# Projecting the S5 input blocks in pairs, and zeroing the far probabilities' tiles on VectorE

## The chip, the cores and the metric

One core of one Trainium2 chip runs the kernel. The metric is the time of one execution on the device in microseconds (us), as the median of several runs. The engines are named as in the profile: PE is TensorE's matmuls and PEld its weight loads, DVE is VectorE, ACT is ScalarE, POOL is GpSimd, SP is the engine that issues most of the loads. "PEq", "SPq" and so on are the sequencers of these engines.

## What is computed

A decoder trunk of two layers over 1024 positions of width 1024, in fp32. Layer 0 projects its normed input once and feeds 16 heads of dilated attention and a multi-scale pooling; layer 1 feeds a chunked spatial gating unit and an S5 state-space layer. After each mixer comes a cross-attention into 256 memory tokens. Cut to what the change touches:

```python
# layer 0: attention, a mixture of three (window, dilation) patterns
A_PATTERNS = ((128, 1), (512, 4), (2048, 16))
a_out = dilated_attention(q, k, v) * silu(g_a)
# layer 1
hn = rms_norm(x, norm_cd)
u_c, v_c, g_c, x_d, g_d = split(hn @ w_in_cd)          # x_d: 512 channels
c_out = spatial_gating(u_c, v_c, ...) * silu(g_c)
d_out = s5_ssm(x_d, ...) * silu(g_d)                    # per group of 16 channels a complex state of 64
y = concatenate([c_out, d_out]) @ w_out_cd
```

## The kernel before

Activations lie with channels on the partitions and 1024 positions on the free axis, in two halves of 512. Every fp32 operand of a large product is split into a rounded part and a rest (`hilo`, and `split` for weights), and each product is three matmuls (`mm3`, L206 to L208). A projection (`proj`) of one block of 128 output channels over one half is 8 x 3 matmuls of 128x512 into one PSUM tile; the PSUM tags have two buffers each ("mm", "s", "o", "t"). An RMS norm is not applied to the input of a projection: the gain is, and the scale 1/rms of each half, `R[0]` and `R[1]`, is multiplied in when the projection is evicted. The sum for the scale is formed by two matmuls with ones (`norm_sum_pe`, L310 and L311), and VectorE then computes the scale by three Newton steps (`norm_sum_end`, `rsqrt`, L289 to L293).

Weights are loaded by SP in the order of a plan (`plan`), split by ACT and DVE some places ahead (`pump`, counted from the oldest weight in use), and freed after their second half (`proj` with h = 1). SBUF tiles come from rings that are shared by many names: 42 buffers of 1024 columns (tag "b") and 14 of 512 columns (tag "u").

The program is written as generators. `drive` runs a main one (projections) and steps a side one in between (`cd_side` for the S5 blocks, `ab_side` for the attention heads). What is written this way gives each instruction a priority; the order on each engine then comes from a list scheduler that simulates the program and picks what is ready and earliest in priority. In the attention stage TensorE's order is pinned to the written one (`in_order`), apart from the S5 preparation (`s5_prep`), most of which runs on GpSimd in that stage.

Two places matter here.

In `cd_main`, right after the first cross-attention, the four S5 input blocks d0 to d3 are projected (`proj(("cd", 16 + d), h, held)`), each half evicted with `R[h]` into `xd` (L1366); the finished block is stored to DRAM from GpSimd's queue (L1370), and `s5_block` reads it back transposed with eight loads on GpSimd's queue (L1260), multiplies (L1281), scans on DVE, and stores `y` from ACT's queue (L1325), which `cd_main` reads for the gated linear unit (L1453). The sum of the second half's norm is still outstanding when `cd_main` begins: `s.flush(1)` issues `norm_sum_pe` after the first projection and `norm_sum_end` after the second.

In `attn`, `turn(b)` transposes the probabilities of one block of 128 queries. Those of the far patterns are copied by ACT into `PTr` (L621), in part of its rows only, so the tile is zeroed first. That is done when b % 4 is 0, for both heads of a pair: 8 pairs x 2 halves x 2 heads = 32 memsets of 128x512 (L604). `last(half)` multiplies V by `PTr` (L646).

Of the kernel before, what the change touches and what calls it, by code (L numbers as in the profile page):

```python
# [11 lines left out]
ALU = mybir.AluOpType  # L12
# [86 lines left out]
class Prog:  # L99
# [451 lines left out]
    def attn(s, pr):  # L551

        nc = s.nc
        q, kk, ga = s.pair[pr]
        V, Vp = s.b("V"), s.b("Vp")
# [7 lines left out]
        P, PT, o, PTr = {}, {}, {}, {}  # L563
# [34 lines left out]
        def turn(b):  # L598
            half, b4 = b // 4, b % 4
            n2, kt = 32 * (b + 1), half + 1  # L600
            if b4 == 0:
                for e in range(2):
                    PTr[half, e] = s.b("PTr") if kt == 2 else s.u("PTr")
                    nc.gpsimd.memset(PTr[half, e][:, 512 * half:512 * half + 512], 0.0)  # L604
            for e in range(2):
                t = P.pop((b, e))
                pt = s.ps("t")
                nc.tensor.transpose(pt[:, :128], t[:, n2:n2 + 128], s.ident)
                for k in range(kt):

                    nc.tensor.transpose(pt[:, 128 + 128 * k:256 + 128 * k], t[:, 128 * k:128 * k + 128], s.ident)  # L611

                if b % 2 == 0:
                    PT[b // 2, e] = s.u("PT")
                c0, j0 = 256 * (b % 2), 1 if b == 0 else 0
                src = bass.AP(tensor=pt.tensor, offset=pt.offset, ap=[pt.ap[0], [0, 2 - j0], [1, 128]])
                nc.vector.tensor_tensor(PT[b // 2, e][:, c0 + 128 * j0:c0 + 256].rearrange("p (j i) -> p j i", i=128), src,  # L617
                                        s.cst[:, C_NM + 128 * j0:C_NM + 256].rearrange("p (j i) -> p j i", i=128), op=ALU.mult)
                for k in range(kt):
                    w = min(128, n2 - 128 * k)  # L620
                    nc.scalar.activation(PTr[half, e][:w, 512 * k:512 * k + 512].rearrange("p (r b i) -> p r b i", r=4, b=4)[:, :, b4, :],  # L621
                                         pt[:w, 128 + 128 * k:256 + 128 * k].rearrange("p (r i) -> p r i", r=4), AF.Copy)
# [15 lines left out]
        def last(half):  # L638
# [15 lines left out]
            if half:  # L654
                s.pair.pop(pr)
                s.attn_done = pr

        return front, turn, mix, last

    def put_g(s, k, h, g):  # L660
# [695 lines left out]
    def cd_main(s):  # L1356
        nc = s.nc
        V = nc.vector
        s.gd, s.xsc, s.yd, s.s5_done = {}, {}, {}, False
        held = {}  # L1360
        for d in range(4):
            x = s.b("xd")
            for h in range(2):
                yield from s.proj(("cd", 16 + d), h, held)
                s.flush(1)
                s.anchor = V.tensor_tensor(x.rearrange("p (j c) -> p j c", j=8)[:, :, 64 * h:64 * h + 64],  # L1366
                                s.last.rearrange("p (c j) -> p j c", j=8), s.R[h].rearrange("p (c j) -> p j c", j=8), op=ALU.mult)
                yield 1
            t = s.dt(f"xd{d}", [128, 1024])
            nc.gpsimd.dma_start(t, x)  # L1370
            s.xsc[d] = t
        s.sgu_prep()
        vh = [s.b("vh") for _ in range(8)]
        stt_ = s.u("stats")
# [1 line left out]
        for ch in range(2):  # L1376
            keys = [("vc", 4 * ch + j) for j in range(4)]
            W = {}
            for tt in range(8):
                p = s.pm()  # L1380
                h, o = tt // 4, 128 * (tt % 4)
# [30 lines left out]
        for ct in range(8):  # L1412
# [14 lines left out]
            for h in range(2):  # L1427
                p = s.ps("t")
# [22 lines left out]
        for d in range(4):  # L1451
            y = s.b("yT")
            nc.gpsimd.dma_start(y, s.yd[d])  # L1453
            for ih in range(2):
                t = s.b("yr", F32R)
                s.hilo(t[:, :512], t[:, 512:], y[:, 512 * ih:512 * ih + 512])
                yT[d, ih] = (t[:, :512], t[:, 512:])
        for ot in range(4):
# [5 lines left out]
            for ih in range(2):  # L1464
                ps = []
                for w in range(2):
                    p = s.ps("ms"[w] * (2 - w))
# [5 lines left out]
                f = lambda v: v.rearrange("p (c i) -> p i c", i=8)[:, 4 * ih:4 * ih + 4, :]  # L1473
# [145 lines left out]
```

## Time and profile before

| what | value |
|---|---|
| time, median of 3 runs | 2037.13 us (2034.31 to 2039.85) |
| the profiled execution | 2035.52 us, of which its span is 2033.8 us |
| PE, DVE, ACT, POOL busy | 99%, 56%, 40%, 28% of the span |
| DMA | 127 GB/s mean |

The span goes from the first to the last instruction of the profiled execution. Stages, read from the lines in order of time: to about 200 us the memory tokens are folded into the weights, to 780 us the attention layer's projections with the heads, the pooling and the S5 preparation, to 900 us its output projection, to 1272 us the first cross-attention with its output product, then the layer with gating and S5, its output projection, and the second cross-attention to the end.

### The profile page before, as it was taken

To read this page: it belongs to the slowest core of one execution; us is meant where nothing else is said; L and a number is where in the kernel's file an instruction comes from. 1 tells how busy PE (TensorE), PEld (TensorE's weight loads), DVE (VectorE), ACT (ScalarE), POOL (GpSimd) and SP (SyncE) were. 2 spreads that over 40 slices of the span, in tenths; PEclk is the share of its full clock that TensorE was granted. 3 is DMA by queue.
4 is the path that set the end of the run, shared out by engine and by line. 5 is a ranking of instruction groups with operands and counts; after the bars stand their busy time and mean duration, and the time that the engine had idled before them with its cause. 6 is when DMAs were issued, how large, how long until landed. Compare 5 with 4: busy or idle time off the path is not lost.

```text
span 2033.8 us, 31759 instructions
## 1 busy us (share of the span) xinstructions
PE 2007.1 (99%) x12294; PEld 1672.7 (82%) x12294; DVE 1139.0 (56%) x2011; ACT 803.6 (40%) x1625; POOL 571.3 (28%) x829
## 2 busy tenths in 40 slices
PE   8999999999999999999999999999999999999998
PEld 7999877777787768888888888788888888888888
DVE  7686055655666685555445557644653334655544
ACT  7776134455345452123333444122221133434454
POOL 4564007932344373231111013211211101220013
PEclk9999999999999999999999999999999999999999
DMA  7988302213122222236533145423322225641142
GB/s 290 309 311 284 99 25 70 71 56 122 53 85 83 71 74 96 86 123 232 183 130 125 42 169 187 152 83 103 125 83 78 75 91 189 199 159 62 65 161 83
DMA packets 129160, 258.67 MB, mean 127 GB/s; under 512 B 12785, under 2 KB 58993, under 8 KB 129009
## 3 DMA queue, kind: packets, MB, share of 16 engines
q1 hardware_dynamic: 86032, 188.47, 27.6%
q0 software_dynamic: 13440, 43.53, 5.8%
q10 hardware_dynamic: 29536, 24.65, 3.8%
q8 instruction: 96, 1.57, 0.3%
q14 instruction: 56, 0.45, 0.1%
HBM read 193.16 MB, written 63.44 MB: 126 GB/s over the span
## 4 chain that ended last, share of the span: by engine, by line
PE 94%; DVE 2%; ACT 1%; DMA 1%; POOL 1%; issue 0%; ACTq 0%; SPq 0%; DVEq 0%; POOLq 0%
PE ps_mm L206 14%; PE ps_mm L208 14%; PE ps_mm L207 14%; PE ps_s L207 5%; PE ps_s L208 5%; PE ps_s L206 5%; PE ps_o L206 4%; PE ps_o L207 4%; PE ps_o L208 4%; PE ps_s L577 2%; PE ps_mm L1390 1%; PE ps_mm L1392 1%; PE ps_mm L1391 1%; PE ps_o L634 1%; PE ps_o L893 1%; PE ps_o L891 1%
## 5 line engine op out<-in xcount | busy, mean ns | idle before, releaser
L181 DVE TENSOR_TENSOR wl<-wst,wh 128x1024 fp32r<-128x1024 f32 (+1 forms) x263 | 348.8, 1340 | 87.4 <-ACT wh L180 79.6
L206 PE MATMUL ps_mm<-xg,wh 128*128 128x512 f32 x928 | 368.8, 397 | 1.2 <-DVE xd L1366 1.2
L208 PE MATMUL ps_mm<-xg,wl 128*128 128x512 f32 x928 | 361.8, 390 | 0.0
L207 PE MATMUL ps_mm<-xg,wh 128*128 128x512 f32 x928 | 361.8, 390 | 0.0
L180 ACT ACTIVATE wh<-wst 128x1024 fp32r<-128x1024 f32 (+1 forms) x263 | 262.8, 1016 | 112.2 <-PE ps_mm L207 96.9
L206 PEld LDWEIGHTS ps_mm<-xg,wh 128*128 128x128 f32 x928 | 174.2, 188 | 44.4 <-issue 7.7
L208 PEld LDWEIGHTS ps_mm<-xg,wl 128*128 128x128 f32 x928 | 174.2, 188 | 37.1 <-issue 0.2
L207 PEld LDWEIGHTS ps_mm<-xg,wh 128*128 128x128 f32 x928 | 174.4, 188 | 34.0 <-issue 0.2
L243 POOL TENSOR_TENSOR acc<-acc,sq 128x512 f32<-128x512 f32 (+1 forms) x81 | 104.6, 1292 | 196.0 <-ACT sq L239 190.9
L226 ACT ACTIVATE xg<-x,gains 128x512 fp32r<-128x512 f32 x64 | 46.1, 721 | 235.4 <-DVE x L831 182.1
L589 ACT ACTIVATE P<-P,mx 128x192 f32<-128x192 f32 (+7 forms) x128 | 66.1, 517 | 142.9 <-DVE mx L588 138.3
L621 ACT ACTIVATE PTr<-ps_t 128x128 f32<-128x128 f32 (+2 forms) x192 | 40.2, 268 | 119.9 <-DVE PT L617 117.5
L227 DVE SCALAR_TENSOR_TENSOR xg<-x,gains,xg 128x512 fp32r<-128x512 f32 x64 | 57.6, 900 | 42.0 <-ACT xg L226 42.0
L584 DVE TENSOR_TENSOR P<-ps_s,cst 128x320 f32<-128x320 f32 (+7 forms) x128 | 65.6, 549 | 15.5 <-PE ps_s L577 6.7
L1418 DVE TENSOR_TENSOR ug<-ps_mm,R 128x512 f32<-128x512 f32 x32 | 22.1, 689 | 89.1 <-PE ps_mm L208 89.0
L617 DVE TENSOR_TENSOR PT<-ps_t,cst 128x256 f32<-128x256 f32 (+1 forms) x128 | 46.1, 399 | 41.6 <-PE ps_t L611 32.4
L206 PE MATMUL ps_s<-gr,wh 128*128 128x512 f32 x168 | 65.5, 390 | 0.0
L208 PE MATMUL ps_s<-gr,wl 128*128 128x512 f32 x168 | 65.5, 390 | 0.0
L207 PE MATMUL ps_s<-gr,wh 128*128 128x512 f32 x168 | 65.4, 389 | 0.0
L591 ACT ACTIVATE P<-P,den 128x192 f32<-128x192 f32 (+7 forms) x128 | 61.3, 511 | 7.6 <-DVE den L590 7.4
L239 ACT ACTIVATE sq<-x 128x512 f32<-128x512 f32 (+1 forms) x77 | 44.7, 582 | 43.0 <-DVE x L939 36.4
L213 ACT ACTIVATE pt<-ps_t 128x128 fp32r<-128x128 f32 x128 | 34.7, 276 | 66.4 <-DVE pt L214 45.5
(455 smaller groups left out, 4912.4 us busy)
## 6 DMA issues: line engine op xcount, KB each, us to landing
wst<-w_ab SPq DMA_DIRECT2D x40, 512.0 KB, 3.8
wst<-w_out_ab SPq DMA_DIRECT2D x32, 512.0 KB, 3.8
wst<-vsc SPq DMA_DIRECT2D x32, 512.0 KB, 3.8
wst<-w_kv SPq DMA_DIRECT2D x31, 512.0 KB, 6.4
wst<-w_cd SPq DMA_DIRECT2D x24, 512.0 KB, 3.4
wst<-w_out_cd SPq DMA_DIRECT2D x32, 384.0 KB, 3.4
wst<-w_q SPq DMA_DIRECT2D x16, 512.0 KB, 6.8
msc<-mo ACTq DMA_DIRECT2D x32, 256.0 KB, 6.7
```

Of the source, the lines that this page charges most:

```text
L180: s.last_hi = s.nc.scalar.activation(H[:, :w], t[:, :w], AF.Copy)
L181: s.nc.vector.tensor_tensor(L[:, :w], t[:, :w], H[:, :w], op=ALU.subtract)
L206: s.nc.tensor.matmul(ps, lhsT=lh, rhs=rh, start=(i == 0), stop=False)
L207: s.nc.tensor.matmul(ps, lhsT=lh, rhs=rl, start=False, stop=False)
L208: s.nc.tensor.matmul(ps, lhsT=ll, rhs=rh, start=False, stop=(i == n - 1))
L226: nc.scalar.activation(H, x, AF.Copy, scale=g)
L227: nc.vector.scalar_tensor_tensor(L, x, g, H, op0=ALU.mult, op1=ALU.subtract)
L243: nc.gpsimd.tensor_tensor(st["acc"][:, :n], st["acc"][:, :n], q[:, :n], op=ALU.add)
L584: nc.vector.tensor_tensor(t[:, :n], p[e][:, :n], s.cst[:, m0:m0 + n], op=ALU.add)
L589: j = nc.scalar.activation(t[:, :m], t[:, :m], AF.Exp, bias=mx, accum_out=den)
L591: k = nc.scalar.activation(t[:, :m], t[:, :m], AF.Copy, scale=den)
L617: nc.vector.tensor_tensor(PT[b // 2, e][:, c0 + 128 * j0:c0 + 256].rearrange("p (j i) -> p j i", i=128), src, s.cst[:, C_NM + 128 * j0:C_N ...
```

## The change

Two edits that are independent of each other. The order of the S5 input projections was d0 half 0, d0 half 1, d1 half 0, d1 half 1, and so on; it becomes d0 half 0, d1 half 0, d0 half 1, d1 half 1, and the same for d2 and d3. A block's tile is taken at its first half and stored after its second. And the memset of `PTr` is issued on VectorE (`nc.vector`) in place of GpSimd.

```diff
@@ attn, turn(b)
                 for e in range(2):
                     PTr[half, e] = s.b("PTr") if kt == 2 else s.u("PTr")
-                    nc.gpsimd.memset(PTr[half, e][:, 512 * half:512 * half + 512], 0.0)
+                    nc.vector.memset(PTr[half, e][:, 512 * half:512 * half + 512], 0.0)
@@ cd_main
-        for d in range(4):
-            x = s.b("xd")
-            for h in range(2):
-                yield from s.proj(("cd", 16 + d), h, held)
-                s.flush(1)
-                s.anchor = V.tensor_tensor(x.rearrange("p (j c) -> p j c", j=8)[:, :, 64 * h:64 * h + 64],
-                                s.last.rearrange("p (c j) -> p j c", j=8), s.R[h].rearrange("p (c j) -> p j c", j=8), op=ALU.mult)
-                yield 1
-            t = s.dt(f"xd{d}", [128, 1024])
-            nc.gpsimd.dma_start(t, x)
-            s.xsc[d] = t
+        xs = {}
+
+        for d, h in [(d + i, h) for d in (0, 2) for h in range(2) for i in range(2)]:
+            if h == 0:
+                xs[d] = s.b("xd")
+            x = xs[d]
+            yield from s.proj(("cd", 16 + d), h, held)
+            s.flush(1)
+            s.anchor = V.tensor_tensor(x.rearrange("p (j c) -> p j c", j=8)[:, :, 64 * h:64 * h + 64],
+                            s.last.rearrange("p (c j) -> p j c", j=8), s.R[h].rearrange("p (c j) -> p j c", j=8), op=ALU.mult)
+            yield 1
+            if h:
+                t = s.dt(f"xd{d}", [128, 1024])
+                nc.gpsimd.dma_start(t, x)
+                s.xsc[d] = t
```

## Rows read from the trace of the kernel before

**Rows 1.** The page's first part: busy us (share of the span) xinstructions.

```profile
PE 2007.1 (99%) x12294; PEld 1672.7 (82%) x12294; DVE 1139.0 (56%) x2011; ACT 803.6 (40%) x1625; POOL 571.3 (28%) x829
```

**Rows 2.** Stretches: their us, then PE, PEld, DVE, ACT, POOL busy, PEclk, DMA.

```profile
200.00:770.00 570.00, 564.14 (x4923) 445.39 (x4923) 328.50 (x773) 246.46 (x663) 238.47 (x482) 1.00 0.23 75
715.00:762.00 47.00, 43.68 (x442) 32.49 (x425) 39.48 (x78) 27.75 (x65) 32.90 (x66) 1.00 0.23 80
```

**Rows 3.** Waits of PE, 200 to 1340 us: us in total, times, longest.

```profile
PE ps_t L608 <- ACT PTr L621: 2.0, 3, 1.2
PE ps_o L1204 <- POOL s5W L990: 1.8, 1, 1.8
PE ps_mm L206 <- DVE G L783: 1.3, 1, 1.3
PE ps_mm L206 <- DVE xd L1366: 1.2, 1, 1.2
PE ps_o L1204 <- ACT s5wz L1205: 0.8, 1, 0.8
```

**Rows 4.** PE in order of time, 1277 to 1292: start, us, instruction [idle before].

```profile
1289.20 0.39 PE L208 MATMUL ps_mm<-xg,wl 128*128 128x512 f32 x1
1290.75 0.50 PE L206 MATMUL ps_mm<-xg,wh 128*128 128x512 f32 x1 [1.16 <-DVE xd L1366]
1291.09 0.39 PE L207 MATMUL ps_mm<-xg,wh 128*128 128x512 f32 x1
```

**Rows 5.** DVE in order of time, 1255 to 1345 us.

```profile
1288.86 0.69 DVE L292 SCALAR_TENSOR_TENSOR nt<-nv,nt 128x512 f32<-128x512 f32 x1
1289.63 1.07 DVE L1366 TENSOR_TENSOR xd<-ps_mm,R 128x512 f32<-128x512 f32 x1
1290.61 0.69 DVE L293 SCALAR_TENSOR_TENSOR R<-nt,R 128x512 f32<-128x512 f32 x1
...
1291.94 1.15 DVE L1366 TENSOR_TENSOR xd<-ps_mm,R 128x512 f32<-128x512 f32 x1
...
1303.02 1.21 DVE L181 TENSOR_TENSOR wl<-wst,wh 128x1024 fp32r<-128x1024 f32 x1
```

**Rows 6.** POOL in order of time, 1255 to 1345 us.

```profile
1296.88 4.24 POOL L1260 DMA_DIRECT2D s5U<-xd  x8 [2.94 <-PE ps_mm L208]
```

**Rows 7.** By tile (s5U, y): xcount: duration ns min/median/max, first and last start; shape.

```profile
L1281 PE MATMUL ps_s<-s5U,s5wz x128: 272/273/323, 1311.8 to 1466.8; 128*64 128x128 f32 x128
...
L1325 ACTq DMA_DIRECT2D y<-s5Y x32: 309/442/791, 1336.5 to 1499.1; - x32
L1453 POOL DMA_DIRECT2D yT<-y x4: 537/540/548, 1629.1 to 1652.9; - x4
```

**Rows 8.** Memsets: line 604 as in rows 7; DVE's groups by shape: busy us, mean ns.

```profile
L604 POOL MEMSET PTr<- x32: 515/526/547, 207.6 to 737.6; 128x512 f32 x32
...
L1302 DVE MEMSET HS<- 128x8 f32 x4 | 0.3, 65 | 0.0
L371 DVE MEMSET onef<- 128x128 f32 x1 | 0.2, 165 | 0.9 <-PEq L1611 0.9
```

**Rows 9.** DVE and POOL in order of time, 545 to 556 us.

```profile
546.36 2.34 DVE L587 TENSOR_TENSOR P<-P 128x128 f32<-128x128 f32 x2
546.46 2.10 POOL L990 TENSOR_TENSOR s5W<-s5o,yz 128x1024 f32<-128x1024 f32 x1
...
554.39 0.99 POOL L604 MEMSET PTr<- 128x512 f32 x2
554.93 0.49 DVE L587 TENSOR_TENSOR P<-P 128x128 f32<-128x128 f32 x2
```

**Rows 10.** POOL in order of time, 495 to 560 us.

```profile
521.46 0.53 POOL L604 MEMSET PTr<- 128x512 f32 x1 [16.28 <-PE ps_o L634]
```

**Rows 11.** Waits of DVE, 185 to 770 us, for a buffer to come free.

```profile
DVE PT L617 <- DMA v<-vt: 5.2, 2, 4.0
```

## Prediction

> **What bounds the kernel now.** I read the page's busy times first: TensorE is busy for 2007.1 of 2033.8 us, VectorE for 1139.0 [rows 1]. So an edit that adds no TensorE work can only win back gaps in TensorE's stream, 26.7 us in all, and can only lose by opening new ones. The table of stretches gives the place next: in the attention stage, where the memsets lie, TensorE stands still for 570.00 - 564.14 = 5.9 us, at a granted clock of 1.00 [rows 2]. The list of who waited for whom, cut to TensorE between 200 and 1340 us, names every gap that either edit can reach [rows 3]: 2.0 us in three pieces for the copy of turned probabilities (L621), 1.8 and 0.8 us for the S5 preparation (L990, L1205), 1.3 us for an eviction in the pooling branch (L783), and 1.2 us for the eviction of the S5 input (L1366). That is 7.1 us, 0.35% of the time. The rest of the 26.7 us lies before 200 and after 1340 us, where nothing is edited. I count a difference of over 0.3% (6.1 us of the median) as one that a measurement of this kernel can tell from no change, so the faster side is nearly closed before any edit is priced: almost all of these gaps would have to go.
>
> **Part one, the S5 input in pairs.** The order before is d0 first half, d0 second half, d1 first half, d1 second half. Each projection is 24 matmuls that start 0.23 us apart, 5.4 us, into one of two "mm" PSUM buffers. The stall is visible in the order of time: TensorE's matmul of 1289.20 should be followed at 1289.43, and the next starts at 1290.75 [rows 4]; its successor starts 0.34 us later and not 0.23. So the loss is 1.32 + 0.11 = 1.43 us. The cause is in VectorE's rows [rows 5]. The second half's scale R[1] comes out of a chain of Newton steps that ends with the step of 1290.61; the eviction of d0's second half needs it and starts at 1291.94. All that time it holds one of the two buffers, so TensorE alternates with only the other one, and has to sit through the eviction of 1289.63 (1.07 us, d1's first half, which needs only R[0]).
>
> In the new order d1's first half runs second and d0's second half third. The norm sum for R[1] is still issued after the first projection and its end after the second, so the chain keeps its start and its end. By 1289.4 three projections are done as before, but now the one that waits for R[1] is the youngest, and the buffer of d1's first half came free at about 1284.1 + 1.1 = 1285.2 (its matmuls take the place that d0's second half had, one projection ahead of 1289.4, and its eviction is priced by the row of 1289.63). The fourth projection finds that buffer free at 1289.43. The fifth wants a buffer at 1294.9, and the eviction of 1291.94 is over at 1293.1, 1.8 us ahead. Gain 1.43 us, and nothing is late next. What this rests on is that d1's first half is evicted inside the Newton chain; the row of 1289.63, 0.04 us after its matmuls and between two steps of the chain, shows that the order does slip it in.
>
> The other things that move: the store of d0's block (GpSimd queue) depends on the same R[1] and keeps its time, and with it the eight loads of its transposed form, issued from 1296.9 to 1301.1 [rows 6]; the matmuls that read them start at 1311.8 [rows 7], which leaves 10.7 us for landing. d1's store comes earlier, and if it is issued ahead of those loads it takes one issue of them, 4.24 / 8 = 0.53 us. d2 is complete one projection later (5.4 us), d3 at the same place. The S5 side work is issued a projection later, its loads on SP's queue with it, among the weight loads of the stage; its last result leaves at 1499.1 and is first read at 1629.1 [rows 7], so 130 us cover it. One more weight pair is held open, but the look-ahead counts from the oldest one held, so the split of one later weight moves back by one projection (5.4 us) and no more buffers are wanted than before; all that the next product starts with are split when the split of 1303.02 ends at 1304.2 [rows 5], and that product starts no earlier than five projections after 1290.75, at 1317.9, so 13.7 us cover 5.4. All of these are priced at zero; where that cover were gone, each would cost its own delay, 0.5 to 5.4 us.
>
> **Part two, the memsets.** 32 GpSimd memsets of 128x512, 0.526 us each, go: 16.8 us off GpSimd, which is not the bound. 32 memsets come onto VectorE. The profile of before has only two small ones there, 65 ns for 8 and 165 ns for 128 elements per partition [rows 8]; the line through them gives 65 + 504 x 100/120 = 485 ns for 512, an estimate, 15.5 us in all. VectorE is busy for 328.5 of 570 us in this stage, and goes to about 344. That is hidden wherever VectorE is not in front of TensorE. It is in front in one crowded place: between 715 and 762 us VectorE is busy for 39.5 of 47 us [rows 2], and there the three L608 gaps and the L783 gap stand. Four memsets belong to the last head pair and fall there (GpSimd issued its last at 737.6).
>
> Bounds of this part: below, TensorE's two waits for the S5 preparation go because GpSimd has 16.8 us less to do, -1.8 - 0.8 = -2.6 us; above, all four memsets of the crowded place lie in the chain before TensorE, 4 x 0.485 = +1.9 us. I take +0.5, one of the four in the chain: 28 of the 32 lie where no TensorE gap waits for VectorE, and against the lower end the s5W row of 1.8 us waits for a GpSimd product, not for a memset.
>
> One hope has no place in this sum, that VectorE gets faster because GpSimd leaves it alone. Beside a GpSimd product of two inputs two VectorE maxima (L587) take 2.34 us; beside two GpSimd memsets the same two take 0.49 us [rows 9]. So the two-input work costs VectorE time and stays; the memsets cost it none. The Trainium skill (SBUF — State Buffer, section "Who interferes with whom") says why that would be: a VectorE instruction with two SBUF inputs contends with GpSimd instructions that read SBUF, not with those that only write. The trace agrees, 0.49 against 2.34 us; were it otherwise, 16 pairs would give back up to 16 x 1.85 = 29.6 us of VectorE time, nearly all of it off TensorE's path. The same section says that a VectorE instruction with at most one SBUF input does not contend with GpSimd, which would hold for the new memset; no row of before shows one of this size beside GpSimd work.
>
> **The sum.** 2035.5 us (the profiled execution) - 1.4 + 0.5 = 2034.6 us. That execution is 1.6 us under the median of the three runs; as a median the forecast is 2037.1 - 0.9 = 2036.2 us.
>
> **The rivals.** *Slower: a memset holds up VectorE.* A memset has to wait until its tile's buffer is free, and on GpSimd such waits were long: 16.28 us until a probability buffer had been read by TensorE [rows 10]. If VectorE gets the memset early in its order, everything behind it waits too: evictions of projections, softmax steps, weight splits. TensorE has cover for one projection, 5.4 us, because of the two "mm" buffers; from there each further microsecond is lost. One wait of 16.28 us would cost 16.28 - 5.4 = 10.8 us, with the gain of part one 2037.1 - 1.4 + 10.8 = 2046.5 us; it passes the 0.3% from a wait of about 13 us. The Trainium skill (Perfetto Trace Analysis, section "Tensor Engine Instruction (MATMUL, LD_WEIGHTS)") calls VectorE strictly first in, first out; the trace agrees, as far as its rows run one behind the other [rows 5]. Against the rival: GpSimd was idle, so its order says nothing of how early VectorE would be given the memset, and VectorE's own waits for buffers in this stage are short, the greatest 4.0 us [rows 11], without a TensorE gap. I give it 0.14.
>
> *The S5 gap stays.* If d1's first half is evicted only behind the Newton chain, the fourth projection waits for it: the chain then ends about 1290.3, the evictions at 1291.4 and 1292.5, and TensorE loses 2.0 to 3.1 us where it loses 1.4 now. That is up to +1.7 + 0.5, 2039.3 us. Against it speaks the row of 1289.63. I give it 0.09.
>
> *The attention gaps go too.* A changed order of VectorE and GpSimd could close all five places: 2037.1 - 7.1 = 2030.0 us. For it: each gap is under 2 us and hangs on the order of a few instructions. Against it: VectorE gets more to do in the crowded place, not less. I give it 0.07, and it passes 0.3% only if it is nearly complete.
>
> **How the numbers follow.** The forecast has the remaining 0.70. Its own range is 2037.1 - 1.4 - 2.6 to 2037.1 - 1.4 + 1.9, that is 2033.1 to 2037.6, and with the scatter of the runs (2034.3 to 2039.9, 2.8 us either way) 2030.3 to 2040.4. The faster rival's 2030.0 and the slower one's 2046.5 set the ends that I take, 2030 and 2046; the tails beyond them hold about 0.12. Faster by over 0.3%: 0.04, about half of the third rival. Slower by over 0.3%: 0.12, most of the first. Within 0.3%: 0.84, all the rest.
>
> **What would show it.** In the profile after: no TensorE wait for xd (L1366), and d1's first half evicted near 1284 us; VectorE memsets of about 0.49 us, some 344 us of VectorE in the attention stage, and no wait in front of them over 5 us; TensorE's busy time unchanged at about 2007 us, with the L608 and L783 gaps of the same size or up to 2 us more in total. It is wrong if VectorE stands in front of a memset for more than 5.4 us, if new TensorE gaps appear away from 715 to 762 us and from the S5 input, or if the time leaves 2030 to 2046 us.

## The result and the profile after

| kernel | median of the runs | to before on the same chip (95% interval) |
|---|---|---|
| before | 2036.47 us (2034.31 to 2039.85) | |
| after | 2051.73 us (2048.90 to 2052.40) | 1.0074 (1.0062 to 1.0085) |

The change costs 15 us; the forecast was 2036.2 us, and the upper end of its range 2046. The profiled execution of after took 2052.0 us, of which its span is 2050.3, 16.5 us more than the one of before. TensorE has the same 12294 matmuls, but is busy for longer than in [rows 1]:

```profile
PE 2014.9 (98%) x12294; PEld 1678.9 (82%) x12294; DVE 1148.4 (56%) x2043; ACT 806.2 (39%) x1626; POOL 560.8 (27%) x797
```

So about 8 us went into slower matmuls and 9 us into gaps. The list of who waited for whom names the gaps of TensorE in after (us in total, times, longest; in part). In the kernels with the S5 edit the lines behind it stand 3 to 4 lines lower: the input's eviction L1366 is L1369, the eviction `ug` L1418 is L1422.

```profile
...
PE ps_mm L206 <- DVE ug L1422: 5.4, 2, 4.5
PE ps_s L577 <- DVE P L584: 5.1, 1, 5.1
PE ps_mm L208 <- DVE wl L181: 2.1, 1, 2.1
PE ps_o L1204 <- POOL s5W L990: 1.8, 1, 1.8
...
PE ps_mm L206 <- DVE G L783: 1.3, 1, 1.3
PE ps_t L608 <- ACT P L591: 1.0, 1, 1.0
...
PE ps_t L608 <- ACT PTr L621: 0.3, 1, 0.3
...
```

Two large rows are new, 5.4 and 5.1 us, for evictions and softmax steps that TensorE did not wait for before; so is the row of 1.0 us (L608 for `P`, L591), which is taken up at rest_dve below. The wait for `xd` of [rows 3] is gone, and the three gaps for turned probabilities (2.0 us there) are down to 0.3. The slower matmuls show in the table of stretches (us, then busy us of PE, PEld, DVE, ACT and POOL, PEclk, DMA share, GB/s), of after:

```profile
114.00:117.40 3.40, 3.40 (x16) 3.40 (x17) 3.20 (x10) 1.76 (x4) 1.20 (x1) 0.50 1.04 390
557.70:561.10 3.40, 3.40 (x11) 2.82 (x12) 1.64 (x6) 3.37 (x7) 0.00 (x0) 0.50 0.49 151
728.40:735.20 6.80, 3.92 (x48) 2.64 (x50) 6.40 (x14) 0.58 (x3) 1.34 (x2) 0.50 0.00 0
1441.80:1448.60 6.80, 5.43 (x13) 4.27 (x14) 6.80 (x10) 0.00 (x0) 2.10 (x2) 0.50 0.16 61
```

A granted clock of 0.50 is the lower of TensorE's two levels, 1.2 of 2.4 GHz. In before these same four stretches have 1.00. The third and the fourth follow the two new gaps.

Where the 16.5 us came from can be followed with the start of the k-th matmul of after set against the k-th of before. Losses and gains of a stretch are read in this way further on too:

| between (time in before) | delay grows by | what stands there in after |
|---|---|---|
| 112 and 200 us | +1.9 | clock 0.50 behind a gap of 2.13 us (1.71 in before) |
| 380 and 480 | +1.2 | a new gap of 0.96 us at 393 (L608 for `P`, L591) |
| 545 and 700 | +1.8 | clock 0.50 behind a gap of 1.80 us (1.78 in before) |
| 700 and 725 | +7.2 | a gap of 5.11 us, then clock 0.50 |
| 725 and 775 | -3.0 | the L608 gaps of [rows 3] are gone but for 0.28 us; the L783 gap is as before (1.26 us) |
| 1280 and 1300 | -1.5 | the gap at the S5 input is gone |
| 1300 and 1520 | +8.7 | gaps of 4.48, 0.26 and 0.94 us, clock 0.50 behind the first |
| 1520 and the end | +0.3 | |

**Loss A, at 731 us.** VectorE's window sum of the pooling branch (L751) adds two SBUF tiles. VectorE in order of time (start, us, instruction), first before, then after:

```profile
715.15 4.11 DVE L751 TENSOR_TENSOR win<-vb 128x1023 f32<-128x1023 f32 x1
719.19 0.88 DVE L584 TENSOR_TENSOR P<-ps_s,cst 128x320 f32<-128x320 f32 x2
```

```profile
720.01 10.81 DVE L751 TENSOR_TENSOR win<-vb 128x1023 f32<-128x1023 f32 x1
730.74 0.88 DVE L584 TENSOR_TENSOR P<-ps_s,cst 128x320 f32<-128x320 f32 x2
```

Behind other work the same sum takes 1.22 us. Here it runs beside GpSimd's stream of products of two SBUF tiles (L990, the doubling of `Er` and `Ei` in `s5_prep`). GpSimd before, around the sum's end:

```profile
716.99 1.19 POOL L990 TENSOR_TENSOR s5w<-Ei,trig 128x256 f32<-128x256 f32 x2
718.12 0.99 POOL L604 MEMSET PTr<- 128x512 f32 x2
719.07 0.79 POOL L990 TENSOR_TENSOR Er<-s5w,s5w 128x256 f32<-128x256 f32 x1
```

The sum ends at 719.26; if its 1.22 us of work were done in one piece at the end, they began at 718.04, within 0.1 us of where the memsets begin. In after there are none, and the last row of GpSimd's stream, before GpSimd itself stands for 6.02 us, is

```profile
728.46 1.28 POOL L990 TENSOR_TENSOR Er<-s5w,s5w 128x512 f32<-128x512 f32 x1
```

which ends at 729.74; the sum ends at 730.82, and less its 1.22 us that is 729.60. The masked scores (L584) wait behind it on VectorE, and TensorE for them:

```profile
731.28 1.82 PE L577 MATMUL ps_s<-kk,q 64*32 64x256 f32 x32 [5.11 <-DVE P L584]
```

**Loss B, at 1443 us.** The S5 side work starts a projection later. The state tile `HS` of its block 1 is written (L1306) at 1376.56 us in before:

```profile
1376.56 0.67 DVE L1306 TENSOR_TENSOR HS<-rt 64x508 f32<-64x508 f32 x1
```

and 43 us later in after, of which 7.2 us are the lateness of the whole kernel at 1376 us. VectorE there, with what follows from it:

```profile
1419.32 0.67 DVE L1306 TENSOR_TENSOR HS<-rt 64x508 f32<-64x508 f32 x1
...
1435.63 1.22 DVE L181 TENSOR_TENSOR wl<-wst,wh 128x1024 fp32r<-128x1024 f32 x1 [10.41 <-ACT wh L180]
1437.76 2.36 DVE L181 TENSOR_TENSOR wl<-wst,wh 128x1024 fp32r<-128x1024 f32 x2 [0.91 <-DMA y<-s5Y]
...
1442.43 0.68 DVE L1422 TENSOR_TENSOR ug<-ps_mm,R 128x512 f32<-128x512 f32 x1
```

The chain reads on from row to row. With `HS` late, the product that reads it is late (L1320, at 1425.60), and the stores of its result (ACT's queue, L1325), which left at 1392.53 in before, leave at 1429.55. ACT stands for 3.98 us, while its queue issues them and until one has landed, and so delivers late the rounded weight for which VectorE waits 10.41 us in front of the split of 1435.63. ACT there, then the last store from the chain of what ended last, which lands 4.79 us after 1432.80:

```profile
1429.55 3.69 ACTq L1325 DMA_DIRECT2D y<-s5Y  x8
1433.50 1.15 ACT L1271 ACTIVATE s5T<-s5raw 128x512 f32<-128x512 f32 x2 [3.98 <-DMA y<-s5Y]
```

```profile
1432.80 4.79 DMA y<-s5Y
```

The weight split of 1437.76 waits a further 0.91 us for that store, which by this reading frees its buffer; behind the split stand four S5 products and then `ug`, and TensorE waits for that one:

```profile
1443.17 0.80 PE L206 MATMUL ps_mm<-xg,wh 128*128 128x512 f32 x1 [4.48 <-DVE ug L1422]
```

In the order that the scheduler fixed for VectorE the two kernels differ just there. Before, block 1's `HS` (memset L1302, then L1306) stands ahead of the round of statistics with L1401; after, behind seven of its steps and one more weight split. Each step waits for one projection of V, so they come 5.44 us apart:

```
before:  L181 wl, L1309 rt, L181 wl, L1398, [L1302 HS, L1306 HS, L1311 HS], L1398, L1401, L1398, L1401, ...
after:   L1309 rt, (six pairs L1402, L1405), L1402, L181 wl, L1405, [L1302 HS, L1306 HS, L1311 HS], L1402, ...
```

### The profile page after: what moved, and what is told of

Read it like the earlier page. It is cut to its first block, busy times and chain, and to the rows that moved or that the text cites. A ratio compares the mean times of both kernels' runs of the same rounds, so it can differ in the third digit from the quotient of the medians.

```text
span 2050.3 us, 31716 instructions
## 1 busy us (share of the span) xinstructions
PE 2014.9 (98%) x12294; PEld 1678.9 (82%) x12294; DVE 1148.4 (56%) x2043; ACT 806.2 (39%) x1626; POOL 560.8 (27%) x797
## 4 chain that ended last, share of the span: by engine, by line
PE 86%; DVE 5%; POOL 3%; ACT 2%; DMA 2%; issue 1%; ACTq 0%; SPq 0%; DVEq 0%; POOLq 0%
PE ps_mm L206 12%; PE ps_mm L208 12%; PE ps_mm L207 12%; PE ps_s L207 5%; PE ps_s L208 5%; PE ps_s L206 5%; PE ps_o L206 4%; PE ps_o L207 4%; PE ps_o L208 4%; PE ps_s L577 2%; PE ps_mm L1396 1%; PE ps_mm L1394 1%; PE ps_mm L1395 1%; PE ps_o L893 1%; PE ps_o L891 1%
## 5 line engine op out<-in xcount | busy, mean ns | idle before, releaser
L662 POOL DMA_DIRECT2D gab<-G x32 | 18.4, 577 | 262.9 <-DMA s5par<-s_d 116.2
L584 DVE TENSOR_TENSOR P<-ps_s,cst 128x320 f32<-128x320 f32 (+7 forms) x128 | 65.3, 547 | 15.2 <-PE ps_s L577 7.1
L1422 DVE TENSOR_TENSOR ug<-ps_mm,R 128x512 f32<-128x512 f32 x32 | 22.0, 689 | 87.9 <-PE ps_mm L208 87.9
L591 ACT ACTIVATE P<-P,den 128x192 f32<-128x192 f32 (+7 forms) x128 | 61.2, 512 | 10.3 <-DVE den L590 10.2
L577 PE MATMUL ps_s<-kk,q 64*32 64x256 f32 (+7 forms) x2048 | 57.4, 332 | 5.1 <-DVE P L584 5.1
```

Source lines behind the costliest of these rows:

```text
L577: i = nc.tensor.matmul(p[e][32 * r:32 * r + 32, c], lhsT=q[rows[e], 128 * b + 32 * r:128 * b + 32 * r + 32], rhs=x, start=True, stop=True)
L584: nc.vector.tensor_tensor(t[:, :n], p[e][:, :n], s.cst[:, m0:m0 + n], op=ALU.add)
L591: k = nc.scalar.activation(t[:, :m], t[:, :m], AF.Copy, scale=den)
```

## The experiments

The theory: A and B are two losses, one for each edit. A: the memsets were pauses in GpSimd's stream, and the window sum has to wait for a pause. B: the later side work lets weight splits take the ring's buffers ahead of `HS`, whose late stores then hold up a split. The rivals: for A, that the memsets cost by themselves, on VectorE, in front of TensorE's work; for B, that the new order of the projections (pairs, weights held longer) does the harm, and not the delay.

**The edits apart.** The S5 edit alone, then the memset edit alone.

```diff
 # s5_only: the S5 hunk of the change, and
-                    nc.vector.memset(PTr[half, e][:, 512 * half:512 * half + 512], 0.0)
+                    nc.gpsimd.memset(PTr[half, e][:, 512 * half:512 * half + 512], 0.0)
 # memset_only: the memset hunk of the change alone
```

> Only the S5 input in pairs; the memsets stay on GpSimd. Theory: the two losses of the changed kernel are separate, and this edit owns the one near 1443 us (4.5 us of TensorE waiting for the eviction L1422, 0.9 us more near 1500, and 6.8 us at half clock, worth 3.4 us), against a gain of 1.4 us at the S5 input. So 2036.5 - 1.4 + 4.5 + 0.9 + 3.4 = 2043.9 us, with a TensorE gap of 4 to 5 us before an eviction of ug and no gap of 5 us in the attention stage. Rival: the loss near 1443 us comes from the memsets, which shift the order of all that follows; then this kernel is at 2035 us, 1.4 us under the kernel before.

> Only the memsets on VectorE; the S5 input in the old order. Theory: this edit owns the loss near 731 us, where TensorE waits 5.1 us for the masked scores L584 behind a window sum L751 that takes 10.8 us where it took 4.1 us, plus 6.8 us at half clock (3.4 us); three L608 gaps of 2.0 us in all go in return. So 2036.5 + 5.1 + 3.4 - 2.0 = 2043.0 us. Rival: both losses belong to the S5 edit; then 2036.5 us and a window sum of some 4 us.

Measured: S5 edit alone 2043.89 us, ratio 1.0033 (1.0021 to 1.0044); memset edit alone 2042.81 us, 1.0028 (1.0018 to 1.0037); before on that chip 2036.77. Each has its own loss and not the other's. TensorE in the first, then the window sum in the second:

```profile
1433.39 0.68 PE L206 MATMUL ps_mm<-xg,wh 128*128 128x512 f32 x1 [4.59 <-DVE ug L1422]
```

```profile
719.91 10.78 DVE L751 TENSOR_TENSOR win<-vb 128x1023 f32<-128x1023 f32 x1
```

Their sum, 7.1 + 6.0 = 13.1 us, is 2 us short of the 15.3 of both; the intervals are about 2 us wide to either side, so nothing need be left over.

**Loss A: which memsets.** Only the last head pair's first half (two of 32) on VectorE; then the other 30.

```diff
 # one_pair_dve
-                    nc.gpsimd.memset(PTr[half, e][:, 512 * half:512 * half + 512], 0.0)
+                    (nc.vector if (pr, half) == (7, 0) else nc.gpsimd).memset(PTr[half, e][:, 512 * half:512 * half + 512], 0.0)
 # rest_dve: the same line with nc.gpsimd and nc.vector exchanged
```

> Only two of the 32 memsets go to VectorE, those of the last head pair's first half, which GpSimd issued at 718.1 us in the kernel before. Theory: these two memsets alone were the pause in GpSimd's stream of two-input products in which the window sum could run; without them the sum waits for the end of the stream, so it takes some 10 us and the loss is the whole of the memset edit's, 5 to 7 us (2041 to 2043 us). Rival: the loss is the load of 32 memsets on VectorE, 15.5 us; two memsets are a sixteenth of it, 0.4 us, within the scatter (2036.5 to 2037 us).

> The complement: 30 of the 32 memsets go to VectorE, and the two of the last head pair's first half stay on GpSimd. Theory of the pause: the window sum takes some 4 us again, no gap of 5 us, and the time is that of the kernel before (2035 to 2038 us). Rival, the load on VectorE: nearly the whole loss, 2042 to 2043 us.

Measured: 2039.31 us, 1.0011 (1.0002 to 1.0020), and 2038.85 us, 1.0007 (0.9999 to 1.0016). Both times lie outside what was expected, the first below it and the second above; the sum does what the theory said. With two memsets moved the whole effect on the sum is there; with thirty moved and these two left it is not. The window sum in the first and in the second, with what TensorE shows in the first:

```profile
715.07 10.71 DVE L751 TENSOR_TENSOR win<-vb 128x1023 f32<-128x1023 f32 x1
```

```profile
717.86 4.18 DVE L751 TENSOR_TENSOR win<-vb 128x1023 f32<-128x1023 f32 x1
```

```profile
726.23 1.82 PE L577 MATMUL ps_s<-kk,q 64*32 64x256 f32 x32 [5.01 <-DVE P L584]
```

In VectorE's order the two moved memsets stand behind the sum and the masked scores, so they can't have held these up: for the gap of 5 us the rival falls. The loss is partly given back. Set against before, the matmuls are 7.4 us late behind the gap and the lower clock, and 3.1 us at 775, because the engines that TensorE waited for in [rows 3] have caught up: the L608 gaps are gone and the L783 gap is 0.3 us. The thirty memsets are not free either. Their kernel has the new gap of 0.94 us near 391 and clock 0.50 near 557 us; its interval just includes no change. The new gap, as the same place in after shows, is not a memset's time on VectorE:

```profile
391.34 0.45 DVE L1109 RECIPROCAL s5z<-s5z 128x48 f32<-128x48 f32 x1 [4.97 <-POOL s5z L990]
```

```profile
393.08 0.33 PE L608 MATMUL ps_t<-cst,P 128*128 128x128 f32 x1 [0.96 <-ACT P L591]
```

VectorE stands at a reciprocal of the S5 preparation for GpSimd's result, and two row maxima (L588) of the softmax, which lie ahead of that reciprocal in before, lie behind it here. In all four kernels with thirty or more memsets on VectorE this wait is 4.9 to 5.0 us; in the nine others, with none or two of them there, it is 3.0 us.

**Loss A: a pause put back.** The memsets stay on VectorE; GpSimd zeroes two scratch tiles that are dead by then, at one place of its stream.

```diff
 # memset_pause = memset_only, and in s5_prep
                 tt(O(Er), A(w1), A(w2), SUB)
+                if (o8, lv) == (0, 5):
+                    V.memset(A(w1), 0.0)
+                    V.memset(A(w2), 0.0)
```

> The memsets on VectorE, the S5 input in the old order, and two small GpSimd memsets of scratch columns (128x256 each, which the next level overwrites) in the middle of the S5 preparation's stream of products. Theory: any GpSimd instruction that reads no SBUF lets the waiting window sum in, so it takes 3 to 6 us and not 10.8 us, and the 5.1 us gap shrinks to under 1.5 us; the time is near that with 30 memsets on VectorE, 2036 to 2040 us. Rival: GpSimd has to be free for as long as the sum lasts (1.1 us), and 0.6 us of memsets is too short; then 10 us and 2042 to 2043 us.

Measured: 2041.08 us, 1.0026 (1.0018 to 1.0035). The sum does what the theory says. VectorE, then GpSimd:

```profile
718.54 5.59 DVE L751 TENSOR_TENSOR win<-vb 128x1023 f32<-128x1023 f32 x1
```

```profile
722.31 0.74 POOL L990 TENSOR_TENSOR Ei<-s5w,s5w 128x256 f32<-128x256 f32 x1
722.99 0.31 POOL L1241 MEMSET s5w<- 128x256 f32 x1
```

It ends at 724.13, so its 1.22 us begin at 722.91, with the pause, which comes later in the sum's time than in before. The gap of 5.1 us is gone; but the time was expected at 2040 or less, and it isn't. Instead, TensorE waits 2.33 us for turned probabilities at 733.85, again with the lower clock behind it, and between 700 and 775 us this kernel loses 2.5 us where the memset edit alone loses 4.1. So the pause shortens the sum, which was the question; that it repairs the stage was not shown here.

**Loss B: the delay alone, and the delay undone.** The kernel before with the side work started one step later and the projections unpaired; the S5 edit with the side work stepped more often (0.55 for 0.5 in `drive`); and that rate in the kernel before, as a control.

```diff
 # before_delay1, cd_side
+            if d == 0:
+                yield 1
             yield from s.s5_block(d)
 # s5_rate55 = s5_only, and this line; before_rate55 = before, and this line
-        drive(tc, s.cd_main(), s.cd_side(), 0.5, 0)
+        drive(tc, s.cd_main(), s.cd_side(), 0.55, 0)
```

> The kernel before, with nothing paired and no memset moved, but the S5 blocks' work starting one of its steps later. Theory: the delay alone puts block 1's HS behind the weight splits, so the gap of 4 to 5 us before the eviction of ug comes, with up to 1 us more after it and up to 3.4 us of half clock, without any gain: 2036.8 + 5 to 2036.8 + 9, so 2042 to 2046 us. Rival: the pairing is needed for it; then 2036 to 2038 us.

> The S5 input in pairs, memsets on GpSimd, and the S5 blocks stepped a little more often (0.55 steps for each step of the main work, where it was 0.5), so that block 1's state tile HS comes before the weight splits again in VectorE's order, as in the kernel before. Theory: the loss near 1443 us comes from block 1 being behind those weights for a shared SBUF buffer; then its output leaves near 1395 us and not at 1430 us, the 4.6 us gap before the eviction L1422 is gone, and the time is that of the kernel before less the 1.4 us at the S5 input: 2035 us (2033.5 to 2037.5). Rival: pairing itself costs there (two weight pairs open, evictions later); then the gap stays and the time is 2042 to 2044 us.

> The kernel before with only the side rate of the S5 stage at 0.55 instead of 0.5; the projections stay unpaired. It is the control for s5_rate55. If the rate does nothing by itself, the two gaps of about 1.2 us in front of the input's transposes near 1292 us stay as in the kernel before, no gap of over 1 us opens between 1300 and 1500 us, and the time is 2035.5 to 2037: then what s5_rate55 has over the kernel with the S5 edit alone comes from ending the delay, and its 1 us against the kernel before from the pairing. Rival: the rate by itself shortens or breaks the stage, and the time is off the kernel before by over 2 us.

Measured: 2045.14 us, 1.0045 (1.0032 to 1.0057); 2035.42 us, 0.9999 (0.9990 to 1.0008); 2036.46 us, 1.0001 (0.9993 to 1.0010). The delayed kernel before has the gap, the S5 edit at the higher rate has not, and its `HS` is early again. TensorE in the first, `HS` in the second:

```profile
1435.17 0.79 PE L206 MATMUL ps_mm<-xg,wh 128*128 128x512 f32 x1 [4.44 <-DVE ug L1420]
```

```profile
1375.74 0.67 DVE L1306 TENSOR_TENSOR HS<-rt 64x508 f32<-64x508 f32 x1
```

The delay makes loss B without any pairing, and pairing with its delay undone makes none: the rival for B falls. The control came out as expected; what its text calls two gaps near 1292 us is one of 1.16 us in before, and 1.16 us in the control. In s5_rate55 the input's gap is gone as well (1.5 us between 1280 and 1300, set against before), but the kernel is no faster, since 1.1 us had been lost ahead of it: a gap of 0.76 us for the S5 preparation (L1205) at 490 us is 1.71 us there. It is 0.73 us in the control. Why it grows with the edit and the rate together is not settled.

**Loss B: the buffer.** In the first kernel `HS` gets a tile of its own, and the ring one buffer less (42 to 41), to stay within the memory. In the second the kernel before gets the smaller ring alone.

```diff
 # s5_own_hs = s5_only, and both lines; before_ring41 = before, and the first
-NB = 42
+NB = 41
-        HS = s.b("HS")
+        HS = s.keep("HS", 1024)
```

> The S5 input in pairs, memsets on GpSimd, steps as before (0.5), but HS gets a buffer of its own and the shared ring has 41 buffers in place of 42. Theory: it was the buffer that block 1 waited for; HS is written by about 1390 us, not at 1419 us, and the gap of 4.6 us before the eviction L1422 goes: 2035 to 2039 us, the upper half if 41 buffers cost something elsewhere. Rival: block 1 was late because it was issued late, not for want of a buffer; then HS stays at about 1419 us and the time at 2042 to 2046 us.

> The kernel before with 41 instead of 42 shared buffers and nothing else. The run with a state tile of its own lost the 4.5 us gap near 1440 us and yet stood at 2042.0; its gaps of 3.71 us near 738 us and 1.03 us near 1379 us were put down to the buffer that it had to give up. If that is so, this kernel has gaps of the same size at the same places and takes 2040 to 2043. Rival: the buffer costs nothing, the time is 2036 to 2037.5, and the private state tile itself made the loss.

Measured: 2042.02 us, 1.0029 (1.0018 to 1.0039), and 2046.13 us, 1.0057 (1.0043 to 1.0071). The waits of TensorE in the first, in part:

```profile
PE ps_t L608 <- ACT PTr L621: 5.4, 3, 3.7
...
PE ps_mm L206 <- DVE ug L1422: 0.6, 1, 0.6
```

and in the second, with its block 1:

```profile
PE ps_t L608 <- ACT PTr L621: 5.4, 3, 3.7
PE ps_mm L206 <- DVE ug L1418: 4.8, 1, 4.8
```

```profile
1416.66 0.67 DVE L1306 TENSOR_TENSOR HS<-rt 64x508 f32<-64x508 f32 x1
```

With a tile of its own `HS` of block 1 is written at 1378.07, and the wait for `ug` falls from 4.6 to 0.6 us: it was the buffer that held `HS` back. Over all kernels, `HS` of block 1 is written at 1409 to 1419 us in the four that have the gap in front of `ug` (after, s5_only, before_delay1, before_ring41), and at 1368 to 1385 us in the nine that have not. The time was expected at 2039 at most and came out above it. Part of that the smaller ring costs elsewhere, and the control shows it: taking one buffer from the kernel before brings the same 3.7 us near 740 us. It brings loss B too, with `HS` 40 us late (5.3 us of it the lateness of that kernel as a whole), in a kernel where nothing of the change is done; the expectation of the control, 2040 to 2043 us, had missed this second part. The gap of 1.03 us near 1379 us of s5_own_hs is not in the control, and why that kernel still loses 3.8 us between 1300 and 1520 us is open.

**A version that gains.** The S5 edit at rate 0.55, the memsets left on GpSimd, and pauses in GpSimd's stream at three levels.

```diff
 # best_a = s5_rate55, and in s5_prep
                 tt(O(Er), A(w1), A(w2), SUB)
+                if o8 == 0 and lv >= 4:
+                    V.memset(A(w1), 0.0)
+                    V.memset(A(w2), 0.0)
```

> The S5 edit with side rate 0.55, the memsets of the far probabilities left on GpSimd, and two scratch memsets of 128x256 on GpSimd behind the subtraction of the real part, in the first octave's spans 16 and up. If pauses in GpSimd's stream let VectorE's window sum end, the sum of 4.1 us near 719 us falls to 1.3 to 3 us, the gaps of PE of 2.0 and 1.3 us in front of the transposes between 726 and 762 us shrink, and the time is 2032 to 2035. Rival: the sum falls, but the extra GpSimd instructions change the order planned further on and open other gaps, so that the time is 2035 to 2040.

Measured: 2031.19 us (2029.68 to 2033.56), ratio to before 0.9980 (0.9971 to 0.9989): 4 us under before, where after is 15 us over before, and 0.8 us under the range that was expected. VectorE's window sum, then GpSimd's first added pause:

```profile
716.15 1.82 DVE L751 TENSOR_TENSOR win<-vb 128x1023 f32<-128x1023 f32 x1
```

```profile
716.42 0.47 POOL L990 TENSOR_TENSOR Ei<-s5w,s5w 128x128 f32<-128x128 f32 x1
716.82 0.21 POOL L1241 MEMSET s5w<- 128x128 f32 x1
```

The sum takes 1.8 us and not 4.1, all L608 gaps are gone, and the matmuls win 3.6 us between 700 and 775, where the gaps of [rows 3] stood. A further 1.5 us come at the S5 input, and 1.1 us are lost at 490 us as in s5_rate55. That kernel is the control: it differs by the pauses alone, wins nothing between 700 and 775 us, and stands at a ratio of 0.9999. The pauses without the S5 edit were not run.

## Why the prediction was wrong

- **The S5 gap: right.** The prediction worked out 1.43 us, the matmuls won 1.5. The eviction of d1's first half does slip into the Newton chain. VectorE in after (the scale's steps are L291 to L293, the others evictions):

```profile
1287.26 1.12 DVE L1369 TENSOR_TENSOR xd<-ps_mm,R 128x512 f32<-128x512 f32 x1
...
1293.39 1.12 DVE L1369 TENSOR_TENSOR xd<-ps_mm,R 128x512 f32<-128x512 f32 x1
1294.41 0.70 DVE L292 SCALAR_TENSOR_TENSOR nt<-nv,nt 128x512 f32<-128x512 f32 x1
```

  After is 9.0 us late at this place, so 1293.39 is 1284.4 on the clock of before, where the prediction put it near 1284. The rival "the S5 gap stays" did not happen.

- **The memset on VectorE: right in size, and not what mattered.** The line through the two small memsets of [rows 8] gave 485 ns; all 32 took 485 ns, and VectorE stood for 1.8 us in front of them altogether (after, groups of instructions by shape: busy us, mean ns, idle before):

```profile
L604 DVE MEMSET PTr<- 128x512 f32 x32 | 15.5, 485 | 1.8
```

  So the slower rival, a memset that waits 16 us at the head of VectorE's order, did not happen either (its 16.28 - 5.4 is 10.9, not 10.8, which changes nothing). That 28 of the 32 could cost nothing where they lie was too much: they changed the order near 391 us, and TensorE lost 1.2 us there.

- **"The memsets cost it none": the first step that failed.** The reading of [rows 9] was right: a memset of GpSimd leaves VectorE's two-input work alone, a product of GpSimd slows it. The conclusion that their removal therefore gives or takes nothing was the error. A stretch in which VectorE is not slowed is worth something when the engine on the other side fills it with the work that does slow it, and the two memsets of 718.12 were such a stretch. The row that told it stood in the trace of before: a window sum of 4.11 us that takes 1.22 elsewhere, ending with the memsets. I looked for what VectorE would be given, in the crowded place [rows 2], and not for what it was waiting on. The Trainium skill (SBUF — State Buffer, section "SBUF: two separate sides") says that a VectorE instruction with two SBUF inputs and a GpSimd instruction that reads SBUF exclude one another, and that whichever starts first keeps the other out for its whole instruction. The trace agrees that VectorE waits, and that a memset lets it in; but by one instruction's length the wait would be at most 1.3 us, the longest product there, and in after it went on over thirteen instructions of the stream, 9.6 us. The prediction's "hope" also came true in part, off TensorE's path: VectorE's maxima (L587) take 362 ns on the mean in after between 190 and 790 us and 453 in before, 10 us of VectorE time in all; why is not known.

- **"130 us cover it" and "no more buffers are wanted": the second step that failed.** The delay of the S5 side work was priced by its last result alone, with 130 us between 1499.1 and 1629.1 [rows 7], and the buffers by counting weights. In between, block 1's tile fell behind weight splits that draw on the same 42 buffers, and was written 43 us later. What ran out was the place in the ring, not the time to the reader. The prediction's fallback, that without cover each part would "cost its own delay, 0.5 to 5.4 us", was too low also: the delay cost 8.7 us of the matmuls' time in after, and one step of delay 9.5 us in the kernel before (2045.14 against 2035.68).

- **No term for the clock.** Every gap was priced at its length. The 5.1 us gap delayed the matmuls by 7.2 us and the 4.5 us gap, with its two small followers of 1.2 us, by 8.7, for behind each TensorE ran at a granted clock of 0.50 at first (the stretches to 735.2 and 1448.6 us above). TensorE's busy time, forecast as unchanged at about 2007 us, rose to 2014.9. The trace of before has no row to price it by: past the first 20 us its gaps are at most 1.8 us long, and its clock is 1.00 from 18 to 2024 us.

- **The sum.** -1.5 at the S5 input, +8.7 for loss B, +7.2 - 3.0 for loss A, +1.2 near 390 us, +1.9 and +1.8 for the lower clock at 114 and 557 us, and 0.3 in small pieces make the 16.5, to rounding. Of these last two, the one at 114 us is not the change's: no edited instruction lies ahead of it, and it occurs in some profiles with a gap of 1.8 us and is missing in others with one of 2.2. The one at 557 us follows a gap of 1.80 us in after and is missing behind 1.78 us in before; it is there in memset_only and rest_dve, and not in memset_pause, which has the same 32 memsets on VectorE, so whether the memset edit has a part in it is open. The prediction had listed every gap that the edits could close, 7.1 us, and had a bound for that side; for gaps that the edits could open it had two rivals with a price, the waiting memset and a late eviction at the S5 input, and neither happened. It also listed gaps up to 1340 us alone, since "nothing is edited" behind; the S5 side work runs on behind it, and there stands loss B, the largest term.

## What to carry to other kernels

Before moving work off an engine, look at what its instructions were pauses in: find neighbours that take several times their usual length beside it and see at which row they end. When side work is shifted by even one step, follow the tiles that it draws from shared rings in the order of each engine, and not just the time until its result is read. In this kernel a new gap of some 5 us in a busy TensorE stream cost its length and a further 2 to 3 us behind it, at the lower clock.

## What the runs showed of the hardware

- A VectorE sum of two SBUF tiles beside GpSimd's uninterrupted stream of two-input products took 10.81 us for 1.22 us of work, and it ended 1.08 us after that stream. The three kernels without a GpSimd memset in that stream (after, memset_only, one_pair_dve) all show this, 10.71 to 10.81 us and 1.08 us. In the ten with one it ended 1.14 to 1.16 us after the memset's start, wherever that lay: before 719.26 (718.12), memset_pause 724.13 (722.99), rest_dve 722.04 (720.89), best_a 717.97 (716.82), for instance. What exactly holds it isn't settled, since VectorE is not always shut out: in before, at 721.63 us, two maxima (L587) take 2.17 us in the same stream, and GpSimd's pair of products beside them takes 3.15 us instead of 2.06.
- Gaps of 4.4 to 5.1 us in TensorE's stream were followed by a granted clock of 0.50, for 3.4 us in one case (s5_only) and some 6.8 us in the six others, where the clock had been 1.00. So were the gaps of 3.71 us (s5_own_hs, before_ring41) and 2.33 us (memset_pause); gaps of 1.8 to 2.2 us were followed by it in some executions and not in others.
- Of this program more than of the chip: one buffer less in a ring of 42 costs the kernel before 11 us (2046.13 against 2035.14), more than either edit.
